# Layer 0's first projections: K in blocks of 2, 2, 4, 4, 4, x loaded behind the first modulation steps, and every other K step split into two rounded halves

## The chip, the cores and the metric

The kernel runs on one core of a Trainium2 chip. The metric is the device time of one execution in microseconds (us). Three executions of the kernel before took 2586.03, 2591.96 and 2594.05 us, so the time before is 2591.96 us (the median).

## What is computed

A decoder trunk of two layers over 256 tokens of width 2048, all in float32. Each layer has a token mixer (three groups of heads that share one wide input projection `w_in`) and a gated feed-forward network. Ahead of each stands a normalisation whose scale and shift come from a conditioning vector `c` by a matrix `w_mod` of 2048 x 12288 per layer:

```
c_act = silu(c)
for l in range(2):
    mod = c_act @ w_mod[l] + b_mod[l]
    shift1, scale1, gate1, shift2, scale2, gate2 = split(mod, 6)
    h = rms_norm(x, norm1_gain[l]) * (1 + scale1) + shift1
    x = x + gate1 * token_mixer(h, ...)          # h @ w_in[l] ... @ w_out[l]
    h = rms_norm(x, norm2_gain[l]) * (1 + scale2) + shift2
    x = x + gate2 * ((silu(h @ w_gate[l]) * (h @ w_up[l])) @ w_down[l])
return rms_norm(x, final_norm_gain)
```

## The kernel before

The tokens lie as two blocks (`blk`) of 128. A product `h @ w` takes the transposed, modulated h (128 of the 2048 K values on the partitions, 128 tokens wide) as the stationary operand and 128 rows of w as the moving one, up to 512 columns at a time, and sums over 16 K steps in PSUM. There are two ways to do a K step, chosen in `stream` by the argument `whole`:

- **whole**: the float32 weights go into the product as they were loaded. Each 512-column product shows as two matrix instructions in the trace. Nothing but TensorE works on such a step. The raw tile rotates through three tags (`raw`, `wh`, `wl`) of three buffers each.
- **split**: ScalarE rounds the weights to a shorter format (`wh`, L328), VectorE takes the rest (`wl`, L329), and TensorE makes three products, h-high by wh, h-high by wl, h-low by wh. The load may use the three `raw` buffers alone.

**Modulation on VectorE.** `mod_segment` makes a piece of `mod`. Its steps each load some rows of `w_mod` by SyncE's queue (L218) and add `c_act[k] * row` to an accumulator with one SCALAR_TENSOR_TENSOR on VectorE (L221). For shift1 and scale1 of layer 0 a step is 128 rows of 512 columns (256 KB), 16 steps make 512 columns of one of the two, and the two alternate. A finished segment is summed over the partitions by four transposes on TensorE (L246) and a reduction on VectorE (L248), and gives the columns that ScalarE uses as scale and bias in `norm` (L456). The later parts of `mod` take steps of 1024 columns (512 KB) in two buffers `mraw`.

**The order.** The modulation steps stand in one queue `mods`. `tick` is called after each K step of a product and takes steps off that queue at a given rate (3.3 per 1024 weight columns in layer 0's first projections, 1.6 in the last of their K blocks, since gate1 and what follows are closed until then); `need` takes as many as are missing when a column is asked for. A scheduler then fixes the order on each engine; SyncE's queue issues nearly all loads, in one order, and each waits for its buffer.

**Layer 0's first projections.** `K_BLOCKS = (4, 4, 4, 4)` cuts the 16 K steps into four blocks, so that TensorE can begin when the first 512 columns of shift1 and scale1 are known. For each block: `norm` of both token blocks for these K values, then the projections qk (1024 columns), z (520), v with the keys and values of the window attention (768), and bq (1024) over the block's K steps. The partial sums are kept in SBUF: the first block copies them there by ScalarE, each later block adds to them by VectorE (`land`, L977). All steps are whole: `WHOLE_IN[0]` is true. In the last block the gated delta rule (`gdn`, many small dependent operations on TensorE, VectorE and ScalarE) is emitted ahead of bq. Then follow the window attention, the projections of the gated linear attention (first three K steps whole, the others split), that attention, `w_out`, and the feed-forward network.

**The start.** Before any modulation step the kernel loads constants, `c`, positions, x (2 MB in one transfer, L193), the gains and small tables, and computes the rotary sines and cosines on VectorE (L176 to L190).

Of the kernel before, what the change touches and what calls it, by code (L numbers as in the profile page):

```python
# [19 lines left out]
P = 128  # L20
D = 2048
# [24 lines left out]
WHOLE_OUT = ((0, 1, 2, 3), ())  # L46
# [57 lines left out]
def trunk(ctx: ExitStack, tc, x, cT, pos, small, consts, b_mod, w_mod, w_in, w_gk, w_out,  # L104
# [22 lines left out]
    def tl(pool, shape, tag, dt=F32, bufs=None):  # L127
        return pool.tile(shape, dt, tag=tag, name=nm(tag), bufs=bufs)
# [25 lines left out]
    c_raw = tl(kp, [P, KD], "c_raw")  # L154
# [19 lines left out]
    SY.dma_start(pos_i, pos)  # L174
    pos_f = tl(kp, [P, NB], "pos_f")
    V.tensor_copy(pos_f, pos_i)  # L176
    ang = tl(kp, [P, NB, 8], "ang")
    V.tensor_tensor(ang, bc(pos_f, 8, 2), bc(cst("freq"), NB, 1), ALU.mult)
    trig = {}
    for name, turn in (("sin", 0.0), ("cos", 0.25)):  # L180
        n = tl(kp, [P, NB, 8], "turns" + name)
        V.tensor_scalar(n, ang, float(1.0 / TWO_PI), turn, ALU.mult, ALU.add)
        V.tensor_scalar(n, n, 12582912.0, -12582912.0, ALU.add, ALU.add)
        r = tl(kp, [P, NB, 8], "trig" + name)
        V.scalar_tensor_tensor(r, n, -PI_HI, ang, ALU.mult, ALU.add)
        V.scalar_tensor_tensor(r, n, -PI_MID, r, ALU.mult, ALU.add)
        V.scalar_tensor_tensor(r, n, -PI_LO, r, ALU.mult, ALU.add)
        V.tensor_scalar(r, r, float(TWO_PI * turn), 3.1415925, ALU.add, ALU.min)
        V.tensor_scalar(r, r, -3.1415925, None, ALU.max)
        A.activation(r, r, AF.Sin)  # L190
        trig[name] = r

    SY.dma_start(xs, x.rearrange("(b p) d -> p b d", p=P))  # L193
# [274 lines left out]

    small_t, wgk_t = {}, {}
    gains = tl(kp, [P, DEPTH, 2 * KD], "gains")  # L470
    SY.dma_start(gains, small[:, :, :2 * KD].rearrange("l p n -> p l n"))

    def load_small(l):
        small_t[l] = tl(kp, [P, SMALL_W], "small")
# [481 lines left out]

    def layer(l):
        wi, wo = w_in[l], w_out[l]
        load_small(l)
# [81 lines left out]

        def project(name):
            segs, at = groups[name]
            gemm(segs, ks, lhs, land(first, last, at), whole=ks if WHOLE_IN[l] else (),
                 lead=ahead(*LEAD_IN) if l and name == "qk" else ())

        for blk in range(NB):
            if l == 0:
                for j in range(4):
                    square(blk, j)  # L1050
            rms[blk] = inv_rms(blk)
        for bi, ks in enumerate(blocks):
# [6 lines left out]
            for name in ("qk", "z", "v"):  # L1059
                project(name)  # L1060
            if l == 0 and first:
                for o in range(0, n_mask, 512):
# [163 lines left out]
```

## Time and profile before

| | us |
|---|---|
| median of three runs | 2591.96 |
| the profiled execution, its own time | 2591.34 |
| its span in the trace | 2589.6 |
| TensorE busy in the span | 2436.7 (94%) |
| VectorE busy | 1752.0 (68%) |
| ScalarE busy | 1067.0 (41%) |
| DMA, moved in all | 600.79 MB |
| granted TensorE clock, mean | 0.986 |

A row of the profile names the line of the kernel, the engine, the operation, the tile written and the tiles read, with shapes. In the timeline the first number is the start, the second the length, and "x8" means that eight like instructions were merged. A busy time of TensorE includes instructions that overlap in its pipeline, so costs on it are read from one start to the next. PEld is the loading of the stationary operand, SPq SyncE's DMA queue. A view by windows gives for each engine its busy time and instructions in a stretch of the span, then the granted clock, the share of time the DMA engines were busy, and what they moved.

### The profile page before, as it was taken

Reading aid. Unit: us, or ns where it says so; the run is one execution under the profiler, and the core shown is the slowest. Engines: PE = TensorE matmul, PEld = TensorE weight load, DVE = VectorE, ACT = ScalarE, POOL = GpSimd, SP = SyncE. Lnnn points to the kernel's source line nnn. Section 1 sums busy time; section 2 is a strip of 40 time slices with the busy share of each in tenths; the row PEclk is TensorE's granted clock in tenths of the full one; section 3 lists DMA queues with packets and bytes.
Section 4 is the critical chain, followed back from the end, with each engine's and each line's share of the span. In section 5 each row is a group of like instructions: output and inputs, shape, how many; then the busy total and the mean of one; then the engine's idle time right before and its main releaser. Section 6 shows DMA issues by size and latency. Waiting matters only on the chain.

```text
span 2589.6 us, 31057 instructions
## 1 busy us (share of the span) xinstructions
PE 2436.7 (94%) x11164; PEld 1885.3 (73%) x11164; DVE 1752.0 (68%) x2527; ACT 1067.0 (41%) x1582; POOL 26.4 (1%) x72
## 2 busy tenths in 40 slices
PE   4999999889999999999999999999899999999997
PEld 2555785447788777788767788877688878888876
DVE  7767876777666777657578788688664575544555
ACT  2203454134444333443445464654544434344443
POOL 0000000000000000000000000000000000000000
PEclk9999999999999999999999999999999999999999
DMA  9986548768778888868687875365676676566654
GB/s 336 367 314 215 179 141 274 270 198 283 261 258 277 280 277 278 279 192 297 217 282 233 283 227 157 96 197 187 213 251 194 204 275 194 188 193 188 188 179 155
DMA packets 190035, 600.79 MB, mean 232 GB/s; under 512 B 21628, under 2 KB 26268, under 8 KB 189496
## 3 DMA queue, kind: packets, MB, share of 16 engines
q1 hardware_dynamic: 189880, 598.81, 70.3%
q8 instruction: 87, 1.43, 0.2%
q14 instruction: 68, 0.56, 0.1%
HBM read 596.63 MB, written 2.10 MB: 231 GB/s over the span
## 4 chain that ended last, share of the span: by engine, by line
PE 54%; DMA 22%; DVE 13%; issue 8%; ACT 3%; SPq 0%; DVEq 0%; POOL 0%; ACTq 0%; POOLq 0%
PE acc L356 47%; DMA mraw<-in_w_mod 12%; DVE wl L329 4%; DVE acc L221 3%; DMA raw<-in_w_down 3%; DMA raw<-in_w_in 2%; DMA raw<-in_w_up 2%; DMA raw<-in_w_gate 2%; ACT wh L328 1%; PE mm L401 1%; PE ga L401 1%; PE ga L901 1%; PE mm L688 1%; DVE g L221 1%; PE ga L924 1%
## 5 line engine op out<-in xcount | busy, mean ns | idle before, releaser
L356 PE MATMUL acc<-wh,hm 128*128 128x512 f32 (+3 forms) x4872 | 1344.2, 389 | 19.7 <-ACT wh L328 6.2
L328 ACT ACTIVATE wh<-raw 128x1024 fp32r<-128x1024 f32 (+3 forms) x669 | 684.4, 1026 | 1022.5 <-PE acc L356 598.2
L329 DVE TENSOR_TENSOR wl<-raw,wh 128x1024 fp32r<-128x1024 f32 (+3 forms) x669 | 785.1, 1179 | 447.1 <-ACT wh L328 445.5
L356 PEld LDWEIGHTS acc<-wh,hm 128*128 128x128 f32 x4872 | 895.0, 189 | 215.5 <-issue 20.0
L356 PE MATMUL acc<-wl,hm 128*128 128x512 f32 (+3 forms) x2484 | 796.9, 395 | 9.0 <-DVE wl L329 6.7
L221 DVE SCALAR_TENSOR_TENSOR acc<-mraw,c_act,acc 128x1024 f32<-128x1024 f32 x320 | 410.3, 1282 | 225.3 <-DMA mraw<-in_w_mod 222.7
L356 PEld LDWEIGHTS acc<-wl,hm 128*128 128x128 f32 x2484 | 458.3, 190 | 119.2 <-DVE wl L329 18.0
L356 PE MATMUL acc<-wh,ahl 128*128 128x512 f32 x560 | 158.9, 397 | 0.2 <-ACT wh L328 0.2
L356 PEld LDWEIGHTS acc<-wh,ahl 128*128 128x128 f32 x560 | 106.1, 190 | 25.1 <-ACT wh L328 0.6
L221 DVE SCALAR_TENSOR_TENSOR g<-g,c_act,g 128x512 f32<-128x512 f32 x128 | 89.0, 746 | 11.2 <-DMA g<-in_w_mod 11.1
L356 PE MATMUL acc<-wl,ahl 128*128 128x512 f32 x280 | 91.3, 400 | 4.8 <-DVE wl L329 4.7
L356 PE MATMUL acc<-wh,b 128*128 128x512 f32 (+2 forms) x184 | 73.8, 540 | 3.3 <-ACT b L456 2.1
L356 PE MATMUL acc<-wl,b 128*128 128x512 f32 (+2 forms) x176 | 66.1, 513 | 1.8 <-DVE g L977 1.8
L356 PEld LDWEIGHTS acc<-wl,ahl 128*128 128x128 f32 x280 | 52.3, 189 | 20.7 <-DVE wl L329 9.2
L356 PE MATMUL acc<-raw,b 128*128 128x512 f32 (+2 forms) x176 | 66.8, 518 | 0.0
L356 PEld LDWEIGHTS acc<-wh,b 128*128 128x128 f32 x184 | 34.7, 195 | 32.6 <-issue 23.7
L456 ACT ACTIVATE b<-mm,mod,mod 128x128 f32<-128x128 f32 x24 | 9.2, 461 | 111.0 <-DVE mod L254 93.5
L356 PEld LDWEIGHTS acc<-wl,b 128*128 128x128 f32 x176 | 32.6, 190 | 29.0 <-issue 21.6
L356 PEld LDWEIGHTS acc<-raw,b 128*128 128x128 f32 x176 | 32.6, 190 | 26.6 <-issue 22.6
L937 DVE TENSOR_TENSOR acc<-acc,gate 128x512 f32<-128x512 f32 x64 | 42.9, 692 | 9.9 <-PE acc L356 9.2
L356 PE MATMUL acc<-raw,hm 128*128 128x512 f32 x88 | 42.9, 611 | 2.9 <-ACT acc L425 2.9
L939 DVE TENSOR_TENSOR xs<-xs,acc 128x512 f32<-128x512 f32 x64 | 42.3, 679 | 0.0
(329 smaller groups left out, 1663.6 us busy)
## 6 DMA issues: line engine op xcount, KB each, us to landing
mraw<-in_w_mod SPq DMA_DIRECT2D x320, 512.0 KB
raw<-in_w_down SPq DMA_DIRECT2D x176, 512.0 KB
raw<-in_w_gate SPq DMA_DIRECT2D x160, 512.0 KB
raw<-in_w_up SPq DMA_DIRECT2D x160, 512.0 KB
raw<-in_w_in SPq DMA_DIRECT2D x72, 512.0 KB
g<-in_w_mod SPq DMA_DIRECT2D x128, 256.0 KB
raw<-in_w_out SPq DMA_DIRECT2D x43, 512.0 KB
raw<-in_w_in SPq DMA_DIRECT2D x32, 264.0 KB
```

The lines of the kernel that those rows point to most:

```text
L221: V.scalar_tensor_tensor(acc, raw[:, a], c_act[:, i + a:i + a + 1], acc, ALU.mult, ALU.add)
L328: A.activation(wh[:, :width], raw[:, :width], AF.Copy)
L329: V.tensor_tensor(wl[:, :width], raw[:, :width], wh[:, :width].bitcast(F32), ALU.subtract)
L356: TE.matmul(ps[blk, j][:, :segs[j][2]], xa, parts[j][part], start=i == 0 and n == 0, stop=last and n == len(terms) - 1)
L401: TE.transpose(ps[:, j * P:(j + 1) * P], src[:, j * P:(j + 1) * P], ident)
L456: A.activation(h32[:, i], ps[:, i * P:(i + 1) * P], AF.Identity, scale=mod_col[l, 3 * sub + 1, at + i], bias=mod_col[l, 3 * sub, at + i])
L688: TE.matmul(ps[:, s], LT[blk][:, s], Tm[blk][:, s], start=True, stop=True)
L901: TE.matmul(ps[:, j * nk:(j + 1) * nk], qT[rows, i + j], kT[rows, g, :nk], start=True, stop=True)
L924: TE.matmul(ps[:, j * 64:(j + 1) * 64], pT[:, j * nk + kb * P:j * nk + (kb + 1) * P], kv[kb][:, P + g * 64:P + (g + 1) * 64], start=kb == ...
L937: V.tensor_tensor(ps, ps, need(gate_row, (l, part, j)), ALU.mult)
L939: V.tensor_tensor(x_j, x_j, ps, ALU.add)
```

## The change

- `K_BLOCKS` becomes (2, 2, 4, 4, 4): five blocks, the first two of two K steps.
- For a block of two, `first_segment` takes the place of two `mod_segment`s. One step loads 128 rows of 256 columns of shift1 and the same 256 of scale1 side by side (256 KB, in runs of 1 KB), and one SCALAR_TENSOR_TENSOR of 512 columns adds both. 16 steps serve a block, and one set of four transposes and one reduction finish it.
- `WHOLE_IN[0]` becomes the odd K steps. The even ones (8 of 16) are split.
- x is loaded in two halves, the first behind four of the first block's 16 modulation steps, the second behind four more; constants and gains come behind that. The small tables, the positions and the rotary computation move behind the first block's qk, z and v.

The diff, with unchanged bodies cut:

```
-K_BLOCKS = (4, 4, 4, 4)
+K_BLOCKS = (2, 2, 4, 4, 4)
...
-WHOLE_IN = (True, False)
+WHOLE_IN = ((1, 3, 5, 7, 9, 11, 13, 15), ())
...
-    SY.dma_start(ct, consts[:, :N_FULL])
...
-    pos_i = tl(kp, [P, NB], "pos_i", I32)
...
-    SY.dma_start(xs, x.rearrange("(b p) d -> p b d", p=P))
+    def rotary():
+        pos_i = tl(kp, [P, NB], "pos_i", I32)
...
+    def first_segment(k0):
+        width = 2 * P
+        st = {}
+
+        def mods_at(w):
+            return w[:, :2 * D].rearrange("p (s n) -> p s n", s=2)[:, :, k0 * P:k0 * P + width]
+
+        def step(i):
+            if i == 0:
+                st["acc"] = scr[1]()
+                G.memset(st["acc"], 0.0)
+                SY.dma_start(st["acc"][0:1].rearrange("p (s n) -> p s n", s=2),
+                             mods_at(b_mod[0:1]))
+            acc = st["acc"]
+            raw = scr[1]()
+            SY.dma_start(raw.rearrange("p (s n) -> p s n", s=2),
+                         mods_at(w_mod[0, i * P:(i + 1) * P]))
+            V.scalar_tensor_tensor(acc, raw, c_act[:, i:i + 1], acc, ALU.mult, ALU.add)
+            if i + 1 == KD:
+                fins.append([FIN_LAG, lambda: finish(acc)])
+
+        def finish(acc):
+            t = tl(smp, [P, 4], f"modfirst{k0}")
+            ps = tl(psf, [P, 512], "fin")
+            for i in range(4):
+                TE.transpose(ps[:, i * P:(i + 1) * P], acc[:, i * P:(i + 1) * P], ident)
+            V.tensor_reduce(t, ps.rearrange("p (a b) -> p a b", a=4), AX.X, ALU.add)
+            V.scalar_tensor_tensor(t[:, 2:], t[:, 2:], 1.0, gains[:, 0, k0:k0 + 2],
+                                   ALU.add, ALU.mult)
+            for j in range(2):
+                mod_col[0, SHIFT1, k0 + j] = t[:, j:j + 1]
+                mod_col[0, SCALE1, k0 + j] = t[:, 2 + j:3 + j]
+
+        return [((0, SHIFT1), lambda i=i: step(i)) for i in range(KD)]
...
     for n in K_BLOCKS:
-        for pair in zip(*(mod_segment(0, part, k0, n) for part in (SHIFT1, SCALE1))):
-            mods.extend(pair)
+        if n == 2:
+            mods.extend(first_segment(k0))
+        else:
+            for pair in zip(*(mod_segment(0, part, k0, n) for part in (SHIFT1, SCALE1))):
+                mods.extend(pair)
...
-            gemm(segs, ks, lhs, land(first, last, at), whole=ks if WHOLE_IN[l] else (),
+            gemm(segs, ks, lhs, land(first, last, at), whole=WHOLE_IN[l],
...
+        if l == 0:
+            for blk in range(NB):
+                for _ in range(4):
+                    mods.popleft()[1]()
+                SY.dma_start(xs[:, blk], x[blk * P:(blk + 1) * P])
+            SY.dma_start(ct, consts[:, :N_FULL])
+            SY.dma_start(gains, small[:, :, :2 * KD].rearrange("l p n -> p l n"))
...
             if l == 0 and first:
+                load_small(l)
+                rotary()
```

SyncE's queue from its first row. Before (xs is x, g a buffer for modulation rows or an accumulator, consts, gains and small the tables):

```order
L151 DMA consts_88<-in_consts 128x392
L155 DMA c_raw_91<-in_cT 128x16
L174 DMA pos_i_102<-in_pos 128x2
L193 DMA xs_93<-in_x 128x2x2048
L471 DMA gains_129<-in_small 128x2x32
L475 DMA small_131<-in_small 128x330
L477 DMA wgk_133<-in_w_gk 16x256
L211 DMA g_221<-in_b_mod 1x512
L218 DMA g_224<-in_w_mod 128x512
```

And now:

```order
L154 DMA c_raw_90<-in_cT 128x16
L215 DMA g_135<-in_w_mod 128x2x256
L211 DMA g_132<-in_b_mod 1x2x256
L215 DMA g_138<-in_w_mod 128x2x256
L215 DMA g_141<-in_w_mod 128x2x256
L215 DMA g_144<-in_w_mod 128x2x256
L1091 DMA xs_92<-in_x 128x2048
L215 DMA g_148<-in_w_mod 128x2x256
L215 DMA g_151<-in_w_mod 128x2x256
L215 DMA g_154<-in_w_mod 128x2x256
L215 DMA g_157<-in_w_mod 128x2x256
L1091 DMA xs_92<-in_x 128x2048
```

Four modulation steps stand ahead of each half of x, and the tables come later.

VectorE where the first block's modulation columns are finished. Before (fin is the PSUM tile of the transposes, mod the columns, hm the rounded halves of h):

```order
L248 TENSOR_REDUCE sums_86_321<-fin_322 128x4
L251 COPY mod_0_4_85_320<-sums_86_321 128x4
L248 TENSOR_REDUCE sums_90_333<-fin_334 128x4
L221 SCALAR_TENSOR_TENSOR g_373<-g_376,c_act_100,g_373 128x512
L254 SCALAR_TENSOR_TENSOR mod_0_4_89_332<-sums_90_333,gains_129 128x4
```

And now (wl_268 is the split of the first weight tile raw_265):

```order
L226 TENSOR_REDUCE modfirst_60_241<-fin_242 128x4
L365 TENSOR_TENSOR wl_268<-raw_265,wh_267 128x1024
L227 SCALAR_TENSOR_TENSOR modfirst_60_241<-modfirst_60_241,gains_101 128x2
L217 SCALAR_TENSOR_TENSOR g_287<-g_290,c_act_99,g_287 128x512
L486 TENSOR_SCALAR b_256<-xs_92,rms_45_198 128x256
```

One reduction serves shift and scale, and a split of weights now stands between it and the finished scale.

TensorE in the first block's qk, for one of the two token blocks. Before, a whole K step (acc are the PSUM sums, b is h in full float32):

```order
L356 MATMUL acc_365<-wh_363,b_211 128x512
L356 MATMUL acc_366<-wh_363,b_211 128x512
L356 MATMUL acc_369<-wh_363,b_347 128x512
L356 MATMUL acc_370<-wh_363,b_347 128x512
L356 MATMUL acc_365<-wl_388,b_211 128x512
```

And now, the end of K step 0 (split) and K step 1 (whole):

```order
L392 MATMUL acc_279<-wh_267,hm_254 128x512
L392 MATMUL acc_280<-wh_267,hm_254 128x512
L392 MATMUL acc_279<-wl_268,hm_254 128x512
L392 MATMUL acc_280<-wl_268,hm_254 128x512
L392 MATMUL acc_279<-wh_267,hm_255 128x512
L392 MATMUL acc_280<-wh_267,hm_255 128x512
L392 MATMUL acc_271<-wh_299,b_209 128x512
L392 MATMUL acc_272<-wh_299,b_209 128x512
L392 MATMUL acc_279<-wh_299,b_253 128x512
L392 MATMUL acc_280<-wh_299,b_253 128x512
```

A split step has three products where a whole one has one, and the two kinds alternate.

More of the change, by code (lines that the diff above doesn't have):

```diff
@@ L193, in trunk @@
-    SY.dma_start(xs, x.rearrange("(b p) d -> p b d", p=P))
+    trig = {}
+    def rotary():
+        pos_i = tl(kp, [P, NB], "pos_i", I32)
+        SY.dma_start(pos_i, pos)
+        pos_f = tl(kp, [P, NB], "pos_f")
+        V.tensor_copy(pos_f, pos_i)
+        ang = tl(kp, [P, NB, 8], "ang")
+        V.tensor_tensor(ang, bc(pos_f, 8, 2), bc(cst("freq"), NB, 1), ALU.mult)
+        for name, turn in (("sin", 0.0), ("cos", 0.25)):
+            n = tl(kp, [P, NB, 8], "turns" + name)
+            V.tensor_scalar(n, ang, float(1.0 / TWO_PI), turn, ALU.mult, ALU.add)
+            V.tensor_scalar(n, n, 12582912.0, -12582912.0, ALU.add, ALU.add)
+            r = tl(kp, [P, NB, 8], "trig" + name)
+            V.scalar_tensor_tensor(r, n, -PI_HI, ang, ALU.mult, ALU.add)
+            V.scalar_tensor_tensor(r, n, -PI_MID, r, ALU.mult, ALU.add)
+            V.scalar_tensor_tensor(r, n, -PI_LO, r, ALU.mult, ALU.add)
+            V.tensor_scalar(r, r, float(TWO_PI * turn), 3.1415925, ALU.add, ALU.min)
+            V.tensor_scalar(r, r, -3.1415925, None, ALU.max)
+            A.activation(r, r, AF.Sin)
+            trig[name] = r
```

21 lines of the change are left out of this document (2 added, 19 removed).

## The prediction

> **What bounds the kernel now.** I read first the view by windows, to see which engine is full where the change works. Columns: stretch, length, then busy us and instructions of TensorE, its weight loads, VectorE, ScalarE and GpSimd, granted clock, DMA share, GB/s.
>
> ```profile
> 0.00:42.00 42.00, 3.46 (x13) 2.26 (x13) 29.81 (x78) 11.81 (x27) 4.59 (x24) 1.00 0.92 321
> 20.00:30.00 10.00, 0.00 (x0) 0.00 (x0) 9.91 (x20) 0.00 (x0) 0.00 (x0) 1.00 0.95 313
> 37.00:42.00 5.00, 2.12 (x9) 1.32 (x8) 3.42 (x8) 0.63 (x2) 0.00 (x0) 1.00 1.03 388
> 42.00:188.00 146.00, 144.76 (x438) 79.10 (x438) 100.25 (x163) 23.22 (x56) 2.71 (x16) 1.00 0.95 344
> 138.00:150.00 12.00, 11.99 (x29) 5.08 (x28) 10.58 (x16) 0.00 (x0) 0.00 (x0) 1.00 1.04 399
> 186.00:260.00 74.00, 69.85 (x246) 38.90 (x245) 58.27 (x186) 27.04 (x56) 0.95 (x1) 1.00 0.68 228
> 260.00:280.00 20.00, 17.64 (x95) 13.46 (x96) 19.21 (x47) 8.01 (x20) 0.00 (x0) 0.93 0.47 135
> ```
>
> Up to 42 us TensorE has next to nothing to do and the DMA is full. From 42 to 188 TensorE idles 1.2 us in all, so it sets the pace, but the DMA is nearly full too (0.95). VectorE is at 69%.
>
> The timeline shows the two ends of that stretch: x's load, the modulation sums on VectorE, the second set of transposes, the first product, and where the last of the four K blocks begins.
>
> ```profile
> 2.11 0.43 SPq L193 DMA_DIRECT2D xs<-in_x  x1
> ...
> 22.47 14.91 DVE L221 SCALAR_TENSOR_TENSOR g<-g,c_act,g 128x512 f32<-128x512 f32 x22
> ...
> 36.78 1.11 PE L246 MATMUL fin<-consts,g 128*128 128x128 f32 x4 [17.91 <-DVE g L221]
> 38.68 1.11 PE L246 MATMUL fin<-consts,g 128*128 128x128 f32 x4 [0.79 <-DVE sums L248]
> 41.88 2.07 PE L356 MATMUL acc<-wh,b 128*128 128x512 f32 x2 [2.09 <-ACT b L456]
> ```
>
> ```profile
> 186.53 1.02 PE L356 MATMUL acc<-wh,b 128*128 128x512 f32 x2
> 188.80 2.84 PE L356 MATMUL acc<-wh,b 128*128 128x512 f32 x6 [1.25 <-DVE b L977]
> 191.48 3.60 PE L356 MATMUL acc<-wl,b 128*128 128x512 f32 x8
> 194.91 3.60 PE L356 MATMUL acc<-raw,b 128*128 128x512 f32 x8
> ```
>
> The first product starts at 41.88 us, 4.5 us behind the last sum (22.47 + 14.91 = 37.38). The last K block starts at 186.53. So a K block takes (186.53 - 41.88) / 3 = 48.2 us. I forecast the moment at which the last block starts in the changed kernel. Everything behind it hangs on that moment by order and waits, with nothing tied to an absolute time, so an earlier start is handed on to the end.
>
> **The change part by part.**
>
> *The start.* Ahead of the first product the DMA must now bring 16 steps of 256 KB (4.19 MB), x (2.10 MB), constants and gains (0.23 MB) and the first weight tile (0.52 MB): 7.04 MB. At 313 GB/s, the row in which modulation rows flowed alone, that is 22.5 us, from 2.1 us on: 24.6 us. Behind it stands the chain of 4.5 us. One set of transposes goes (1.9 us, 36.78 to 38.68), one split of the weights comes in on VectorE ahead of the scale (1.2 us, row below), so I keep 4.5: 29.1 us.
>
> The new steps read runs of 1 KB where the old ones read 2 KB, and no row shows such loads by themselves. Below nothing the price cannot go, since no load gets shorter. At the other end, if the queue were bound by runs, a segment would take twice its 4.19 / 0.313 = 13.4 us. The same 2 KB runs went at 313 GB/s in one stretch and made up most of the 388 in another, so runs were hardly what bound the 313; I take 2 us for each of the two segments, partly behind the 4.5 us: first product at 29.5 us, 12.4 earlier.
>
> The Trainium skill (DMA: Bandwidth & Descriptors, Specifications) says that transfers of 512 B and more reach line rate; by that the narrow runs cost nothing and the sum is some 2 us better. The trace agrees only in part: runs of 2 KB lie between 313 and 388 GB/s here.
>
> *Products.* One whole K step costs, from start to start, 3.43 us in qk and as much in bq (191.48 to 194.91), and by these rows 1.76 in z and 2.58 in v:
>
> ```profile
> 69.15 2.74 PE L356 MATMUL acc<-wh,b 128*128 128x512 f32 x8
> 71.73 2.74 PE L356 MATMUL acc<-wl,b 128*128 128x512 f32 x8
> ...
> 108.00 1.92 PE L356 MATMUL acc<-wh,b 128*128 128x260 f32 x8
> 109.76 1.92 PE L356 MATMUL acc<-wl,b 128*128 128x260 f32 x8
> ```
>
> That is 11.2 us. A split step is seen in the feed-forward network, six products for one token block:
>
> ```profile
> 701.00 0.62 PE L356 MATMUL acc<-wl,hm 128*128 128x512 f32 x2
> 701.46 1.07 PE L356 MATMUL acc<-wh,hm 128*128 128x512 f32 x4
> 702.36 0.62 PE L356 MATMUL acc<-wl,hm 128*128 128x512 f32 x2
> ```
>
> 1.36 us for six, so 2.72 for 1024 columns and both blocks; by columns 2.72 + 1.38 + 2.04 + 2.72 = 8.9 us. A block of four K steps falls from 44.8 to 40.2 us of products. The measured 48.2 held 3.4 us of other things (transposes, waits); with them 43.6 us.
>
> *VectorE.* These groups give its prices (busy us, mean ns):
>
> ```profile
> L221 DVE SCALAR_TENSOR_TENSOR g<-g,c_act,g 128x512 f32<-128x512 f32 x128 | 89.0, 746 | 11.2 <-DMA g<-in_w_mod 11.1
> L977 DVE TENSOR_TENSOR g<-g,acc 128x512 f32<-128x512 f32 x12 | 8.1, 683 | 2.4 <-PE acc L356 2.3
> ...
> L248 DVE TENSOR_REDUCE sums<-fin 128x4 f32<-128x512 f32 x8 | 5.5, 691 | 13.7 <-PE fin L246 13.7
> L460 DVE TENSOR_TENSOR hm<-b,hm 128x512 fp32r<-128x512 f32 x7 | 4.8, 689 | 5.6 <-ACT hm L459 5.6
> L450 DVE TENSOR_SCALAR b<-xs,rms 128x512 f32<-128x512 f32 x8 | 3.8, 479 | 0.0
> L977 DVE TENSOR_TENSOR g<-g,acc 128x260 f32<-128x260 f32 x4 | 1.7, 424 | 5.1 <-PE acc L356 5.0
> ...
> L977 DVE TENSOR_TENSOR kv<-kv,acc 128x256 f32<-128x256 f32 x4 | 1.7, 413 | 0.0
> ```
>
> ```profile
> L329 DVE TENSOR_TENSOR wl<-raw,wh 128x1024 fp32r<-128x1024 f32 x13 | 15.8, 1215 | 5.9 <-ACT wh L328 5.9
> L329 DVE TENSOR_TENSOR wl<-raw,wh 128x528 fp32r<-128x528 f32 x16 | 11.2, 702 | 1.6 <-ACT wh L328 1.5
> ```
>
> Between the first product and the start of the last block VectorE now has:
> 112 modulation sums at 0.678 (14.91 / 22, start to start), 76 us; three rounds of adding partial sums instead of two, each 8 x 0.683 + 2 x 1.0 (z, in three pieces) + 2 x 0.413 = 8.3, so 25 us; splits of six K steps, each 1.215 + 0.70 + 0.95 (between the two widths) + 1.215 = 4.1, so 24.5 us; normalising, some 9 us (0.479 + 0.689 for each token block); reductions of 0.691 and what goes with them, 6 us; masks, four casts of at most 0.48, 1.9 us; the rotary computation, 17 instructions of 0.17, 2.9 us, by this row:
>
> ```profile
> 4.33 0.17 DVE L182 TENSOR_SCALAR turnssin<-ang 128x16 f32<-128x16 f32 x1
> ```
>
> That is 145, less 0.07 for each pair that overlaps (0.746 against 0.678), about 140 us. In one block of four it is 32 x 0.678 + 8.3 + 8.2 + 2.3 + 1.7 = 42 us. The rotary work lay in time when VectorE waited for x and cost nothing; now it lies under its full load, and is counted. ScalarE rounds the same weight tiles at about the same price; with 23.2 of 146 us busy it has room.
>
> *DMA.* Ahead of the first block of four must come, behind the 24.6 us: the second narrow segment (4.19 MB and 2 us), the rest of four K steps of w_in (1.71 MB each, 6.3 MB), masks and tables (1.1 MB), and 32 wide steps (8.39 MB): 20.0 MB at 344 GB/s, 58 us. So 84.7 + 4.5 = 89 us. TensorE has only two blocks of two to do until then, 29.5 + 2 x 20.1 + 2 = 72 us: it waits some 17 us. That wait is new, and takes what the first blocks could have gained. Each block of four then needs 8.39 + 6.83 = 15.2 MB, 44 us; only ahead of the last block does the DMA run ahead, by five ticks' worth of w_in (39 ticks of 3.3 steps against 112), 7 us.
>
> *A cold start.* After an idle stretch the first products are slow, as these weight loads show, 0.85 us apart and then 0.43:
>
> ```profile
> 46.31 0.34 PEld L356 LDWEIGHTS acc<-wh,b 128*128 128x128 f32 x1 [0.52 <-issue]
> 47.16 0.34 PEld L356 LDWEIGHTS acc<-wh,b 128*128 128x128 f32 x1 [0.52 <-issue]
> 47.96 0.19 PEld L356 LDWEIGHTS acc<-wh,b 128*128 128x128 f32 x1 [0.46 <-issue]
> 48.39 0.19 PEld L356 LDWEIGHTS acc<-wl,b 128*128 128x128 f32 x1 [0.24 <-issue]
> ```
>
> Four pairs at 0.42 more make 1.7 us, paid once more behind the new wait. The windows' granted clock reads 1.00 there and does not show it. The Trainium skill (TensorE: Matmul & The Clock Gate, Part 1) has TensorE at half clock until it has been busy for about 3.4 us; an estimate from that is also 1.7 us per restart, and the halved spacing agrees.
>
> *The sum.* Start of the last block: by TensorE 89 + 2 x 43.6 + 1.7 = 178; by VectorE 29.5 + 140 / 0.96 (its fullest row, 19.21 of 20) = 175; by the DMA 89 + 2 x 44 - 7 = 170. Three limits this close share some slack, so I take 177, 9.5 us earlier than 186.5.
>
> *The last block.* Two splits save TensorE 4.6 us and give VectorE 8.2. VectorE idled 15.7 of 74 us from 186 to 260, so it has room, barely, once the gated delta rule's small operations mix in: I take half the saving, 2.3 us. The later order is nearly the same, apart from some loads around `w_out`; I give that no price of its own, and 3 us either way.
>
> 2591.3 (the profiled execution's own time, 0.6 below the median of the runs) - 9.5 - 2.3 = **2579.5 us**.
>
> **The rivals.**
>
> *The DMA keeps up its best rate.* At 399 GB/s (the row from 138 to 150) the first block of four is reached at 81, the blocks then go at TensorE's 43.6, and the last starts at 168; with the full 4.6 saved that is 23 us less, 2568. For it: the DMA was at 399 with VectorE at 88%. Against it: the mean over 146 us was 344, since buffers have to come free.
>
> *Narrow runs cost half of their upper bound*, 6.7 us a segment and not 2. The first block of four then comes 9.4 us later, the last block starts where it did, and 2.3 us are left: 2589, no change. The early stretch at 313 GB/s speaks for it, the 388 against.
>
> *VectorE becomes the bound, and the kernel slower.* It works in order, and each modulation sum waits for its load with splits, additions and reductions queued behind it; TensorE waits for the splits and for PSUM to come free, SyncE's queue for the modulation buffers. At 85% the last block starts at 29.5 + 140 / 0.85 = 194, 7.7 us later, and its last two splits cost VectorE 8.2 against 4.6 saved: 2602. It decides from 140 / 157 = 89% downwards. Of its rows 260 to 280 (96%) speaks against it, 138 to 150 (88%) and the 11.1 us of waits for w_mod for it.
>
> **How the numbers follow.** Forecast 0.45, best rate 0.19, narrow runs 0.20, VectorE 0.16. A measurement of this kernel tells about 0.3% (7.8 us) from no change. Faster: 0.19 and 0.42 of the 0.45, 0.61. Within: 0.20 and 0.02, 0.22. Slower: 0.17 with the rest. The range goes from just under the fast rival, 2565, to 2598, which holds the no-change rival and part of the slow one.
>
> **What would show it.** Right: first product near 29.5 us, TensorE idle from about 72 to 89, the last block's first product near 177, VectorE over 90% busy between. Wrong: a first product past 35 us (narrow runs), VectorE under 89% with TensorE waiting for `wl` (the slow rival), or a last block that starts as forecast while the gain is gone by 260 us.

## The result, and the profile after

The changed kernel is **slower**: 2612.17 us (median of four runs, 2606.41 to 2616.15) against 2592.08 for the kernel before on the same chip, a ratio of 1.0079 with a 95% interval of 1.0059 to 1.0100, some 20 us. The forecast was 2579.5. The profiled execution has a span of 2609.2 us (before 2589.6) and a mean granted clock of 0.978 (0.986).

In the changed kernel the product is L392, the rounding L364, the rest `wl` L365, the modulation sum L257 (L217 in the two narrow segments), the weight load L357, the modulation load L254, adding partial sums L1016, the transposes of a finished segment L282. The view by windows, columns as in the prediction:

```profile
20.00:30.00 10.00, 1.22 (x5) 0.82 (x6) 9.16 (x24) 2.08 (x6) 0.00 (x0) 1.00 1.07 368
42.00:188.00 146.00, 121.96 (x453) 80.64 (x453) 124.20 (x214) 37.49 (x66) 3.56 (x18) 0.92 0.89 305
80.00:101.00 21.00, 12.31 (x43) 7.11 (x41) 20.80 (x35) 3.31 (x7) 1.05 (x2) 0.84 0.90 293
101.00:152.00 51.00, 45.74 (x175) 29.86 (x173) 45.50 (x73) 12.66 (x23) 1.45 (x14) 0.97 0.96 343
152.00:200.00 48.00, 45.94 (x172) 31.11 (x173) 35.65 (x55) 10.65 (x15) 0.00 (x0) 0.93 0.81 274
200.00:260.00 60.00, 45.06 (x183) 30.07 (x181) 51.01 (x140) 27.34 (x47) 0.00 (x0) 0.90 0.72 234
```

From 42 to 188 us TensorE was 84% busy (99% before) at a granted clock of 0.92 (1.00), VectorE 85% (69%), and the DMA moved less (305 GB/s, 344 before). No engine is full over the whole stretch. VectorE is full in a part of it: from 80 to 101 us, ahead of the first block of four, it was busy 20.80 of 21. TensorE's timeline:

```profile
30.35 1.22 PE L392 MATMUL acc<-wh,hm 128*128 128x512 f32 x2
...
64.01 2.08 PE L392 MATMUL acc<-wh,hm 128*128 128x512 f32 x4 [2.58 <-ACT wh L364]
...
85.85 3.60 PE L392 MATMUL acc<-wl,b 128*128 128x512 f32 x8
93.57 0.66 PE L282 MATMUL fin<-consts,g 128*128 128x128 f32 x4 [4.13 <-DVE g L257]
95.97 1.11 PE L282 MATMUL fin<-consts,g 128*128 128x128 f32 x4 [1.75 <-DVE sums L284]
99.10 1.12 PE L489 MATMUL ga<-consts,b 128*128 128x128 f32 x4 [2.01 <-DVE b L486]
...
101.28 1.22 PE L392 MATMUL acc<-wh,hm 128*128 128x512 f32 x2
...
151.90 1.84 PE L392 MATMUL acc<-wh,hm 128*128 128x512 f32 x4 [2.54 <-ACT wh L364]
...
200.67 0.98 PE L392 MATMUL acc<-wh,hm 128*128 128x512 f32 x2
```

The first product came at 30.35 us, 11.5 earlier than before. The four K steps of the two small blocks then lasted to 89.3 (85.85 and 3.43). The modulation columns of the first block of four were ready for their transposes only at 93.57 and 95.97, behind VectorE's sums, and that block began at 101.28. The blocks of four took 50.6 and 48.8 us. The last one started at 200.67 us, 14.1 later than before; 177 was forecast.

The view of waits from 30 to 200 us (total, number, longest), TensorE's first, then VectorE's, then the first row of ScalarE's:

```profile
PE acc L392 <- ACT wh L364: 9.8, 5, 4.1
PE acc L392 <- DVE wl L365: 5.9, 8, 1.5
PE fin L282 <- DVE g L257: 4.1, 1, 4.1
```

```profile
DVE wl L365 <- ACT wh L364: 11.0, 5, 3.9
DVE g L1016 <- PE acc L392: 9.6, 11, 3.4
```

```profile
ACT wh L364 <- DMA raw<-in_w_in: 61.7, 12, 14.7
```

TensorE waits for ScalarE and VectorE, and VectorE, when it idles, for ScalarE and TensorE, no longer for loads. ScalarE, whose rounding stands at the head of every split, waits for the loads of the weights.

A second piece was lost in the last block. TensorE's sums of squares and decay matrix of the delta rule, before and after:

```profile
247.30 3.63 PE L601 MATMUL mm<-ones,g 128*128 128x1 f32 x32
...
259.77 2.07 PE L640 MATMUL mm<-g,consts 128*128 128x512 f32 x2 [0.20 <-ACT g L626]
```

```profile
259.13 6.96 PE L639 MATMUL mm<-ones,g 128*128 128x1 f32 x32 [5.53 <-DVE g L595]
...
282.47 1.06 PE L678 MATMUL mm<-g,consts 128*128 128x512 f32 x2
```

The 12.5 us between the two became 23.3. The first lasted twice as long, behind a wait of 5.53 us; and VectorE's chain of small operations between them, here its first step, what comes next, and its end, took 11.9 us (before 4.5), and two splits, four additions and three modulation sums, among others, stand in it:

```profile
266.68 0.17 DVE L444 TENSOR_SCALAR qkrs<-qkss 128x16 int32<-128x16 int32 x1
266.76 1.22 DVE L365 TENSOR_TENSOR wl<-raw,wh 128x1024 fp32r<-128x1024 f32 x1
...
278.55 0.16 DVE L647 TENSOR_TENSOR knorm<-knorm,qkrs 128x8 f32<-128x8 f32 x1
```

At the decay matrix the kernel is 22.7 us late, at the end of the span 19.6: all is lost by 283 us, and 3.1 of it come back behind that.

### The profile page after: what moved, and what is told of

Read it like the earlier page. It is cut to its first block, busy times and chain, and to the rows that moved or that the text cites. A ratio compares the mean times of both kernels' runs of the same rounds, so it can differ in the third digit from the quotient of the medians.

```text
span 2609.2 us, 31468 instructions
## 1 busy us (share of the span) xinstructions
PE 2436.5 (93%) x11292; PEld 1910.4 (73%) x11292; DVE 1793.3 (69%) x2581; ACT 1093.6 (42%) x1615; POOL 26.4 (1%) x72
## 4 chain that ended last, share of the span: by engine, by line
PE 53%; DMA 20%; DVE 12%; issue 10%; ACT 4%; SPq 1%; POOL 0%; DVEq 0%; ACTq 0%; POOLq 0%
PE acc L392 45%; DMA mraw<-in_w_mod 11%; DVE wl L365 5%; DMA raw<-in_w_down 3%; DMA raw<-in_w_in 2%; DVE acc L257 2%; DMA raw<-in_w_gate 1%; ACT wh L364 1%; DMA raw<-in_w_up 1%; PE ga L437 1%; PE mm L437 1%; PE ga L939 1%; PE mm L726 1%; PE ga L962 1%; PE mm L733 1%
## 5 line engine op out<-in xcount | busy, mean ns | idle before, releaser
L392 PE MATMUL acc<-wh,hm 128*128 128x512 f32 (+3 forms) x5136 | 1429.1, 391 | 32.1 <-ACT wh L364 14.7
L364 ACT ACTIVATE wh<-raw 128x1024 fp32r<-128x1024 f32 (+3 forms) x701 | 713.5, 1020 | 1090.4 <-PE acc L392 580.3
L365 DVE TENSOR_TENSOR wl<-raw,wh 128x1024 fp32r<-128x1024 f32 (+3 forms) x701 | 818.3, 1172 | 452.0 <-ACT wh L364 449.8
L392 PEld LDWEIGHTS acc<-wh,hm 128*128 128x128 f32 x5136 | 943.4, 190 | 246.8 <-issue 31.7
L392 PE MATMUL acc<-wl,hm 128*128 128x512 f32 (+3 forms) x2604 | 829.5, 393 | 16.7 <-DVE wl L365 16.0
L392 PEld LDWEIGHTS acc<-wl,hm 128*128 128x128 f32 x2604 | 482.0, 190 | 135.1 <-DVE wl L365 30.3
L257 DVE SCALAR_TENSOR_TENSOR acc<-mraw,c_act,acc 128x1024 f32<-128x1024 f32 x320 | 410.3, 1282 | 197.2 <-DMA mraw<-in_w_mod 194.7
L392 PE MATMUL acc<-wh,ahl 128*128 128x512 f32 x560 | 158.3, 397 | 0.0
L392 PEld LDWEIGHTS acc<-wh,ahl 128*128 128x128 f32 x560 | 106.0, 190 | 24.5
L392 PE MATMUL acc<-wl,ahl 128*128 128x512 f32 x280 | 91.0, 399 | 4.2 <-DVE wl L365 4.0
L257 DVE SCALAR_TENSOR_TENSOR g<-g,c_act,g 128x512 f32<-128x512 f32 x96 | 66.9, 746 | 0.0
L392 PEld LDWEIGHTS acc<-wl,ahl 128*128 128x128 f32 x280 | 52.4, 189 | 19.6 <-DVE wl L365 7.8
L392 PE MATMUL acc<-raw,hm 128*128 128x512 f32 x88 | 43.5, 614 | 0.0
L392 PE MATMUL acc<-wh,b 128*128 128x512 f32 (+2 forms) x96 | 39.4, 546 | 0.0
L392 PE MATMUL acc<-wl,b 128*128 128x512 f32 (+2 forms) x96 | 37.2, 523 | 0.0
L392 PE MATMUL acc<-hm,ahl 128*128 128x512 f32 x120 | 32.3, 407 | 4.0 <-ACT hm L371 2.6
L595 DVE SCALAR_TENSOR_TENSOR g<-mm,small,g 128x253 f32<-128x253 f32 (+2 forms) x72 | 30.5, 475 | 3.0 <-ACT g L592 2.8
L951 ACT ACTIVATE b<-b,neg 128x128 f32<-128x128 f32 (+1 forms) x64 | 28.3, 444 | 10.0 <-DVE neg L948 9.7
```

The source lines that it names most:

```text
L257: V.scalar_tensor_tensor(acc, raw[:, a], c_act[:, i + a:i + a + 1], acc, ALU.mult, ALU.add)
L364: A.activation(wh[:, :width], raw[:, :width], AF.Copy)
L365: V.tensor_tensor(wl[:, :width], raw[:, :width], wh[:, :width].bitcast(F32), ALU.subtract)
L392: TE.matmul(ps[blk, j][:, :segs[j][2]], xa, parts[j][part], start=i == 0 and n == 0, stop=last and n == len(terms) - 1)
L595: V.scalar_tensor_tensor(y[:, c, d:], p3[:, c, :T - d], conv[:, ch * 4 + i:ch * 4 + i + 1], y[:, c, d:], ALU.mult, ALU.add)
L951: A.activation(s[:, j], s[:, j], AF.Exp, bias=neg[:, j:j + 1], accum_out=tot[:, j:j + 1])
```

## The experiments

The ratio is to the kernel before, timed on the same chip. The letters of the theories hold within one group of runs.

| run | what differs | median us | ratio | 95% |
|---|---|---|---|---|
| e1 | blocks 2,2,4,4,4, nothing split | 2596.71 | 1.0026 | 1.0012 to 1.0039 |
| e2 | blocks of four, even steps split | 2605.37 | 1.0060 | 1.0040 to 1.0080 |
| e3 | blocks of four, nothing split | 2583.74 | 0.9971 | 0.9953 to 0.9990 |
| e4 | changed kernel, no rests | 2597.36 | 1.0040 | 1.0020 to 1.0059 |
| e5 | changed, last block whole | 2602.45 | 1.0059 | 1.0038 to 1.0079 |
| e6 | changed, split in the last block only | 2600.37 | 1.0041 | 1.0021 to 1.0061 |
| e7 | changed, `raw` for split steps only | 2616.91 | 1.0108 | 1.0076 to 1.0141 |
| e8 | blocks 2,2,2,2,4,4, nothing split | 2594.93 | 1.0015 | 1.0000 to 1.0030 |
| e9 | blocks of four, steps 5 and 9 split | 2590.34 | 0.9999 | 0.9982 to 1.0017 |
| e10 | e1 with a lower last rate | 2596.95 | 1.0022 | 1.0005 to 1.0039 |
| e11 | e3 with a lower last rate | 2587.30 | 0.9995 | 0.9981 to 1.0009 |
| e12 | changed, rests on GpSimd | 2622.32 | 1.0127 | 1.0100 to 1.0154 |
| e13 | changed, steps written one ahead | 2612.28 | 1.0097 | 1.0081 to 1.0113 |
| e14 | changed, `w_in` on GpSimd's queue | 2607.47 | 1.0082 | 1.0061 to 1.0103 |
| e15 | e9 written one ahead | 2589.96 | 1.0007 | 0.9993 to 1.0022 |
| e16 | e13 and e14 together | 2608.56 | 1.0086 | 1.0070 to 1.0101 |
| e17 | changed, half the sums left out | 2609.52 | 1.0077 | 1.0051 to 1.0103 |
| e18 | e3, half the sums left out | 2587.86 | 0.9998 | 0.9981 to 1.0015 |

### The parts by themselves: e1, e2, e3

```
e1: WHOLE_IN = (tuple(range(16)), ())
e2: K_BLOCKS = (4, 4, 4, 4)
e3: both lines, so that only the moved loads and tables are left
```

> The changed kernel with all K steps of layer 0's first projections whole; blocks 2, 2, 4, 4, 4 and the late x stay. Theory S (the splits are the cost: VectorE works in order, TensorE waits for its halves, and the loads behind it come late): VectorE loses some 24 us of work, the first product stays near 30 us, the first block of four comes near 89, the last block near 186 (two blocks at the old 48.2), and the time falls to 2585 to 2592. Theory B (the blocks of two are the cost: the wait ahead of the first block of four and a round of additions more): the first block of four still comes near 100, the last near 197, and the time is 2602 to 2606.

> The changed kernel with blocks 4, 4, 4, 4; every other K step split, and x behind the first modulation steps. Theory S: the three blocks take some 50 us each from a first product near 42, so the last block starts near 192 and the time is 2597 to 2606. Theory B: the splits pay as TensorE's prices say, blocks of 43.6, the last block near 173, and the time is 2575 to 2585.

> Blocks 4, 4, 4, 4 and all steps whole: of the change only the moved loads of x, constants, tables and the rotary computation are left. Both theories: the same bytes ahead of the first product less the tables, so it starts within 1 us of 41.9, and the time is within 5 us of the kernel before, 2587 to 2595. Outside that, the moved loads have a price of their own that neither theory has.

Against e3 the small blocks cost 13 us (e1), the splits 22 (e2), both 28 (the changed kernel, by the ratios 1.0079 and 0.9971): each part costs by itself, and together less than their sum. Over e1 the splits cost 14. What e1's early start came to stands in its timeline:

```profile
29.16 5.77 PE L392 MATMUL acc<-wh,b 128*128 128x512 f32 x8
...
74.38 3.70 PE L392 MATMUL acc<-wh,b 128*128 128x512 f32 x8
83.23 1.12 PE L282 MATMUL fin<-consts,g 128*128 128x128 f32 x4 [5.15 <-DVE g L257]
...
88.25 2.08 PE L392 MATMUL acc<-wl,b 128*128 128x512 f32 x2 [2.00 <-ACT b L492]
```

It reaches the first block of four at 88.25 us (89 was forecast, for that limit), after a wait of 10 us from 78, and its last block begins with transposes at 184.62, where e3, which starts 11 us later, is at 184.26. With whole steps TensorE has no room to make up anything, so what the small blocks win at the start is given back in that wait. In the changed kernel TensorE reached the end of the small blocks only at 89.3 in place of 78: there the splits cost 10 us where they were to save 4.6. The columns of the first block of four came later by as much, with transposes at 93.57 in place of 83.23.

The small blocks cost in the last block, too. From its first transposes to the decay matrix e1 needs 80.3 us, without a split:

```profile
184.62 0.60 PE L489 MATMUL mm<-consts,b 128*128 128x128 f32 x4
...
264.92 1.02 PE L678 MATMUL mm<-g,consts 128*128 128x512 f32 x2
```

e3 needs 75.2 us for the same way (184.26 to 259.50), the kernel before 73.7, the changed kernel 82.2 (200.32 to 282.47). So more of the 8.6 us that are lost there goes with the small blocks than with the splits.

Of the forecasts, e2's time lies in the range of theory S. e1's time lies between its two ranges, and e3 is faster than its range.

### What in the splits costs: e4, e5, e6, e7

```
e4: in layer 0's first projections no wl is made; the product takes wh in its place
e5: WHOLE_IN[0] also has 12 and 14
e6: WHOLE_IN[0] = all but 12 and 14
e7: whole steps rotate through ((wsp, "wh"), (wsp, "wl")) and leave raw to the split ones
```

> The changed kernel with VectorE's part of the splits of layer 0's first projections left out: the second product takes the rounded weights again in place of their rest, so TensorE, ScalarE and the loads do the same, and those projections are computed less exactly. Theory S in its narrow form (VectorE's own time and order are what the split costs): VectorE has 24 us less to do, TensorE waits no more for the rest, the last block starts near 177 and the time is 2575 to 2585. If instead the loads are the cost (split steps can use three buffers only, and their loads stand in SyncE's queue behind modulation loads that wait for buffers), little changes: 2600 to 2610. Theory B: also 2600 to 2610.

> The changed kernel, but the last K block of layer 0 whole (no splits in K steps 12 and 14). What is to be told apart is where the splits cost. If they cost in the last block too, because VectorE does them among the small dependent operations of the delta rule (V): the last block starts near 200 as in the changed kernel, the way from the sums of squares to the delta rule's first decay matrix (23 us there, 12.5 before) shrinks to some 14 us, and the time is 2602 to 2607. If they cost only ahead of the last block (early): the last block's products get 4.6 us longer and nothing is won, 2611 to 2618.

> Blocks 2, 2, 4, 4, 4 with splits in the last block alone (K steps 12 and 14). The last block starts near 185, as with all steps whole. V: the splits delay the delta rule by some 8 us and save TensorE 4.6: 2598 to 2604. Early: the two splits pay their 4.6 us, 2590 to 2594.

> The changed kernel, with the three raw buffers left to the split steps: whole steps take the six buffers of the other two tags only. If late loads for the splits (a full raw ring ahead of them in SyncE's queue) are what holds TensorE (L): the waits for the rounded weights shrink from 9.8 us, the last block starts 5 to 10 us earlier, 2600 to 2606. If VectorE's order and load are (V): within 4 us of the changed kernel, 2608 to 2616.

By the ratios, 10 us come back without VectorE's rests (e4), with the same number of products, and 4 are left over e1. That is less than e4's theory S had forecast, and more than its rivals; e4's interval ends where that of the changed kernel begins. All of the gain lies behind the start of the first block of four: the transposes of its columns come at 94.17 us in e4 and at 93.57 in the changed kernel, the last block's first transposes at 194.57 and 200.32. The profiled execution of e4 took 2591.74 us, 5.6 less than its median. The two splits of the last block cost 4 us over e1 (e6, intervals overlapping), the six before it 9 (e5): together 13 of the 14. Giving the split steps buffers of their own gained nothing (e7 is slower than both of its ranges). It also left the whole steps six buffers where they had shared nine, so it shows that this division doesn't help, and not that the buffers play no part. The way from the last block's transposes to the decay matrix is 76.2 us in e4, 78.2 in e5 and 81.1 in e6: the two parts of the change do not simply add up there. e5 and e6 have the times that V forecast, but in e6 not by V's way: V had the two splits delay the delta rule by some 8 us, and the way is 0.8 longer than in e1.

### Is it the share of VectorE? e9, e10, e11, e12, e8

```
e8: K_BLOCKS = (2, 2, 2, 2, 4, 4)
e9: e3 with WHOLE_IN[0] = all but 5 and 9
e10, e11: e1 and e3 with RATE_LAST = 1.4
e12: V.tensor_tensor -> G.tensor_tensor for wl, in layer 0's first projections
```

> All steps whole, blocks 2, 2, 2, 2, 4, 4: the step from a block of two to a block of four, at which TensorE waits for twice the modulation columns, comes later, and one more round of partial sums is added on VectorE. If that wait and the cold clock behind it are what eats the early start of the blocks of two: the last block starts 3 to 8 us earlier than 184.6 and the time is 2585 to 2592. If the rounds of additions and the shifted order in the delta rule eat it: 2597 to 2603.

> Blocks of four K steps, x and tables moved, all K steps whole but 5 and 9 (one in the second block, one in the third). Theory V (VectorE's share of the stretch decides what a split is worth): VectorE goes from 70% to about 75% from 30 to 200 us, far from full, so TensorE does not wait and keeps 0 to 2.3 us of each: 2579 to 2584, last block 0 to 4.6 us earlier than 184.3. Rival P (each split costs the same, whatever VectorE has to do, 22 us for eight, so 2.7 each): 2589, last block at 188 or later. Rival D (the DMA sets the start of the last block): no earlier, 2584.

> Blocks 2,2,4,4,4, all steps whole, and modulation steps taken at 1.4 in place of 1.6 in the last block, which shifts the order of what is mixed there and leaves the work the same. Theory O (what the blocks of two lose behind the last block's start is the order in which the scheduler mixes the delta rule with other work): the time moves by 4 us or more, and the difference to the blocks of four with the same rate is no longer 13 us. Rival B (small blocks cost by what they do before the last block, or a busier DMA): 2594 to 2600, with the difference to the blocks of four between 9 and 17.

> Blocks of four, all steps whole, rate 1.4 in place of 1.6 in the last block. Theory O: the time moves by 4 us or more from 2583.7, in either direction. Rival B: 2581 to 2587.

> The changed kernel, with the rest of the split weights (wl) of layer 0's first projections taken by GpSimd in place of VectorE. Theory V (VectorE's work in order is what costs): VectorE falls to about 115 of 170 us; if GpSimd takes twice VectorE's time for it (2.4 us for 1024 columns), its 65 us fit, and the time comes down to 2595 to 2604, short of what leaving the rest out gave (2597) by the longer wait for each. Rival S (ScalarE's rounding and the load's buffers cost, whoever takes the rest): 2608 to 2616. Slower than 2616 if GpSimd needs over four times VectorE's time or holds VectorE up.

e9 went against the theory that a split is free where VectorE has room: VectorE was 73% busy from 30 to 200 us, and the last block's transposes came at 193.21, 9 us behind e3's (184.26) and 10 behind e11's (183.09). How much of that stays in the time isn't settled: by the ratios the two splits cost 7 us over e3 (intervals that overlap a little), but 1 over e11, which was timed with e9 on one chip and differs from e3 only in the last rate. TensorE's timeline at the first split step, qk of K step 5:

```profile
91.02 3.60 PE L392 MATMUL acc<-wl,b 128*128 128x512 f32 x8
...
95.36 1.20 PE L392 MATMUL acc<-wh,hm 128*128 128x512 f32 x4 [0.31 <-ACT wh L364]
97.82 0.85 PE L392 MATMUL acc<-wl,hm 128*128 128x512 f32 x2 [1.25 <-DVE wl L365]
98.47 1.06 PE L392 MATMUL acc<-wh,hm 128*128 128x512 f32 x2
...
101.03 3.50 PE L392 MATMUL acc<-raw,b 128*128 128x512 f32 x7
```

The step lasted 5.67 us (95.36 to 101.03), more than a whole one (3.43), where 2.72 was forecast from the feed-forward network. Behind the waits of 0.31 and 1.25 us the last six products, from 98.47 on, took 2.56 us, where six take 1.36 in the prediction's row, and the granted clock reads 0.76 from 95 to 102. The Trainium skill (TensorE: Matmul & The Clock Gate, Part 1) has half clock follow an idle window of about 3.4 us that runs freely; here 1.6 us of waits were enough, and in the changed kernel as much at 141 to 143 was not:

```profile
140.93 1.19 PE L392 MATMUL acc<-wh,hm 128*128 128x512 f32 x4 [0.36 <-ACT wh L364]
143.36 0.74 PE L392 MATMUL acc<-wl,hm 128*128 128x512 f32 x2 [1.23 <-DVE wl L365]
143.94 0.63 PE L392 MATMUL acc<-wh,hm 128*128 128x512 f32 x2
...
145.33 3.60 PE L392 MATMUL acc<-wh,b 128*128 128x512 f32 x8
```

There, at full rate, the step still took 4.40 us. Where nothing had to be waited for, the changed kernel's products cost what the prediction says:

```profile
156.41 3.59 PE L392 MATMUL acc<-wl,b 128*128 128x512 f32 x8
159.44 1.49 PE L392 MATMUL acc<-wh,hm 128*128 128x512 f32 x4
...
162.60 3.60 PE L392 MATMUL acc<-raw,b 128*128 128x512 f32 x8
```

A whole step and a split one, from 156.41 to 162.60, took 6.19 us together; 3.43 and 2.72 make 6.15. So it is the waits, and the slow products behind some of them, that cost.

e12 kept VectorE as busy as it was (139.4 of 170 us), since GpSimd's rests hold up its sums. The groups of VectorE and of GpSimd from 30 to 200 us, and the line of the sum from 100 to 200 (shortest, median and longest in ns):

```profile
L258 DVE SCALAR_TENSOR_TENSOR g<-g,c_act,g 128x512 f32<-128x512 f32 x96 | 88.3, 969 | 2.7 <-DMA g<-in_w_mod 2.7
```

```profile
L366 POOL TENSOR_TENSOR wl<-raw,wh 128x1024 fp32r<-128x1024 f32 x11 | 28.1, 2552 | 67.1 <-ACT wh L365 54.0 <-DMA g<-in_w_mod 13.0
```

```profile
L258 DVE SCALAR_TENSOR_TENSOR g<-g,c_act,g x64: 734/743/2868, 100.2 to 190.2; 128x512 f32<-128x512 f32 x64
```

A sum took 969 ns on average and not 746, so e12 says nothing on the cause. The rate moved e1 and e3 little, and left 9.7 us between them by the medians, 7 by the ratios (13 and 14 before): that small blocks cost is not an accident of one order, though e8, which has four of them, came out between its two expectations. What costs e1 its 7 to 14 us, when its last block starts with e3's, stays open: 5.4 of them are there at the decay matrix (264.9 against 259.5), the rest behind it.

### Late weights or VectorE's work? e13 to e18

```
e13: parts = load(job n + 1) is written ahead of products(job n)
e14: G.dma_start in place of SY.dma_start for w_in in layer 0's first projections
e15: e9 with e13's edit;  e16: e13 and e14 together
e17, e18: in mod_segment, shift and scale of layer 0, every second sum over 16 columns
          (changed kernel, e3)
```

> The changed kernel, with load, rounding and rest of each of layer 0's first projection steps written one K step ahead of its products. Theory L (the weights of a split step come late, TensorE waits and then runs cold): TensorE's waits for wh and wl from 30 to 200 us fall from 15.7 us to under 8, a block of four from 50.6 and 48.8 us to 47 or less, the time to 2598 to 2607. Rival W (the amount of VectorE's work): 2608 to 2616, since the work is the same.

> The changed kernel, with the loads of w_in in layer 0's first projections issued by GpSimd's queue in place of SyncE's, so that they no longer stand behind modulation loads that wait for VectorE. Theory L: ScalarE's wait for these loads (61.7 us) and TensorE's for wh (9.8) fall by half or more, the time to 2595 to 2605. Rival W: 2608 to 2616. Slower than that if GpSimd's issuing holds VectorE up as its arithmetic did (969 ns a sum in place of 746).

> Blocks of four, all steps whole but 5 and 9, written one step ahead. Theory L: the two splits stop costing, 2580 to 2586 (2590.3 without it, 2583.7 without splits). Rival W: 2587 to 2593.

> The changed kernel with both, one step ahead and the loads on GpSimd's queue. Theory L: the least of the kernels with these blocks and splits, 2588 to 2600, with TensorE's waits for wh and wl under 5 us. Rival W: 2605 to 2616.

> The changed kernel, with every second modulation sum of layer 0's shift and scale from the blocks of four on taken over 16 columns in place of 512, which leaves out that half of the modulation (48 sums of 0.68 us, some 30 us of VectorE, about as much as leaving out the rests took); loads, splits and TensorE's waits for wl stay. Theory W (VectorE's amount of work in order): 2594 to 2603. Theory L (TensorE's waits for each split's weights): 2607 to 2614.

> Blocks of four, all steps whole, with the same half of the modulation sums left out (64 of 128). Theory W: TensorE sets the pace there, VectorE at 70% costs nothing but the start, where half the sums of the first block are saved while loads set the pace: 2578 to 2587 (2583.7 without). If VectorE's work costs in general: under 2575.

e13, e14, e15 and e16 moved nothing that can be told apart by the ratios; e14's median lies just between its two ranges, the others came out as rival W had them. e14's waits of TensorE, the four longest:

```profile
PE mm L490 <- DVE b L487: 7.3, 3, 2.9
PE fin L226 <- DVE g L218: 6.8, 1, 6.8
PE acc L393 <- ACT hm L496: 5.7, 1, 5.7
PE fin L283 <- DVE g L258: 4.5, 1, 4.5
```

With the loads on a queue of their own the waits for `wh` are gone and 0.9 us of those for `wl` are left. In their place TensorE waits as long for what the normalisation and the modulation get from VectorE (146.7 of 170 us busy): without the 6.8 us for the first segment, which lie ahead of 30 us in the changed kernel, the waits add up to some 27 us in both. But e14 isn't a clean test. Its first product came at 35.86 us, 5.5 later than in the changed kernel, and its profiled execution (2617.98 us) was the slowest of six; its first block of four (101.33) and the last block's first transposes (200.60) came when they did in the changed kernel. So a queue of their own for the loads gains nothing as a whole; that late loads cost nothing isn't shown. e17 took the other side away, VectorE's amount of work, but for the two narrow segments, which keep all their sums:

```profile
30.00:200.00 170.00, 147.97 (x546) 97.23 (x546) 121.69 (x245) 48.73 (x88) 3.55 (x18) 0.94 0.90 313
```

```profile
PE acc L393 <- ACT wh L365: 8.5, 4, 4.1
PE ga L490 <- DVE b L487: 4.7, 2, 3.0
PE acc L393 <- DVE wl L366: 4.5, 9, 1.3
```

VectorE is at 72% there, as in e4 (123.7 us), and TensorE waits much as before: the ratio is 1.0077, where e4 has 1.0040. With as much work left on VectorE, some 10 us hang on whether TensorE has to wait for a rest (intervals that overlap a little). The amount of VectorE's work alone is not the cause, and in e18, whose median is 0.9 us above its range, it was worth nothing.

What the runs leave is this: a split makes TensorE's K step wait for ScalarE and then VectorE, whose queue holds additions and reductions that wait for TensorE; none of the remedies that left that tie in place gained (e7, e13, e14, e16 and e17, ratios 1.0077 to 1.0108), and cutting it at the rest gained 10 of 14 us. That the two queues wait for each other is read from the views of waits; no run tested it apart from the rest.

What the splits cost ahead of the first block of four is not cured by e4. The transposes of its columns come at 94.17 us there, at 90.25 in e17, and at 83 to 84 in e1, e6 and e10, whose small blocks have no splits. One step on the way can be read: the transposes of the second narrow segment, for which VectorE's reduction waits, came at 57.39 us in the changed kernel and 58.11 in e4, behind waits of TensorE of 4.10 and 4.69 us for a rounding, and at 51.18 in e1.

In e4 TensorE still waits 11.7 us for `wh`; e4 with the loads on a queue of their own was not run, so whether the other 4 us, and the saving that the splits promised, would come with it stays open.

No version with splits or small blocks beats the kernel before. e3 did, by 0.29% (0.10 to 0.47), but e11 and e18, which should cost no more, stand level with the kernel before; by these three runs the moved loads are worth 0 to 8 us.

## Why the prediction was wrong

**The start** was right: 30.35 us for 29.5. The narrow runs cost nothing to be seen, 368 GB/s from 20 to 30 us against 313 before; the rule cited there from the Trainium skill (DMA: Bandwidth & Descriptors, Specifications) fits this better than the 2 us taken, though weight tiles flowed beside the narrow rows there. The one rate of 313 GB/s held only as a mean: 206 GB/s were moved in the first 10 us and 366 in the next 10.

**The failing step is "The sum", by the term that it takes from "Products": a block of four at 43.6 us of TensorE.** That term has a price for a split's products and none for waiting until the weights are loaded and rounded and their rest is taken; ScalarE was counted as having room, and it did, but it waited 61.7 us for loads. The price of the products held (6.19 us for 6.15 where the weights stood ready). With a wait the qk step read above took 4.40 us in place of 2.72, and one in e9 5.67. The two blocks took 99.4 us and not the 88 between 89 and 177: 11.4 too many, of which TensorE's waits for `wh` and `wl` from 101 to 201 us make 7.1. The other 12.3 were lost ahead of them. "DMA" was right that the first block of four can't begin before 89 (e1: 88.25), but the sum let TensorE do the small blocks in 42.5 us, and with splits they took 58.9; the columns of the next block, which wait for VectorE, came 10.3 us later than in e1. 11.4 and 12.3 are the whole 23.7 between 177 and 200.67. The sum took the latest of three limits, each worked out as if the other engines were ready. With splits they aren't independent. Which of the queues would have to be freed for it is open, as said above.

**"A cold start"** was counted once. The granted clock of 0.92 over 146 us, against 1.00, shows that TensorE lost its rate more than once: behind the wait of 2.54 us at 151.90, for one, the clock reads 0.61 from 152 to 156.4, and then 1.00 to 162.6.

**"VectorE", its work** was sized well: 140 us, and 141.3 from 30 to 200. Its fill was 83%, not 96%.

**"The last block"**: "has room, barely" was wrong. In place of a gain of 2.3 us the way to the decay matrix grew by 8.6. The later order was not "nearly the same", and the smaller blocks alone did most of that: e1, with no split, is 6.6 us longer than the kernel before on this way, the changed kernel 1.9 longer than e1. In the changed kernel splits and additions stand inside VectorE's chain of small operations; what lengthens e1's way wasn't tested. Behind it 3.1 us came back, about the 3 us allowed there.

**The slow rival** had the right place and sign, and its condition (under 89%) was met; it priced the last block at 194 and the end at 2602. Its mechanism was only half right: it made VectorE's throughput the bound, and with VectorE freed in e17 the time stays where it was, within the intervals, while the split still waits in its queue. Ahead of the first block of four VectorE was indeed full (20.80 of 21 us). The best-rate rival fell with 305 GB/s, the narrow-run rival with 368.

## What to carry over

A saving in instructions taken from a stage where operands stand ready doesn't hold in one where they are made just in time: price the chain load, rounding, rest, product with the queues as they stand there, and add what a wait costs behind itself in slow products. An engine that needs little from the others (here TensorE with whole steps) keeps its pace beside a DMA that is 95% busy; once it waits for another queue at every step, the larger of two limits is no longer the time, since, by the views of waits, each waits for the other. An earlier start is worth only what the next limit behind it leaves, which a row for that limit (the columns of the next block, at 88 us) shows beforehand.

## What the runs showed of the hardware

- A GpSimd subtraction of two 128x1024 tiles (2.55 us; 1.22 on VectorE) stopped VectorE's sums: their median stayed at 743 ns, but single ones took up to 2868 ns, and the mean rose from 746 to 969. The Trainium skill (SBUF — State Buffer, SBUF: two separate sides) has a port pair that the two share as a lock for a whole instruction, for a VectorE operation with two inputs from SBUF; the 2868 ns agree: they are 2.1 us more than 743, less than one such GpSimd instruction.
- Waits of 1.6 us in sum halved TensorE's rate for the next 2.6 us in e9, and 1.6 us in the changed kernel (0.36 and 1.23) did not. So their sum alone doesn't decide. Whether the moment at which they fall does, was not tried.
